# One adaLN chunk computed on TensorE in place of VectorE, and the sine layers of the Hyena filters written ahead of all adaLN work

## The chip, the cores and the metric

The kernel runs on one core of one Trainium2 chip. The metric is device time in microseconds (us) of one launch; lower is better. All times below are device times of that one core.

## The reference, cut to what matters

The program is a two-layer encoder trunk over 256 tokens of width 1024. Every layer is an FFN half-step, a mixer (RWKV-7, Hyena long convolution and Mamba-2 side by side) and a second FFN half-step. Each of the three is modulated by a vector that comes from the conditioning `c`:

```
cond = silu(c)
mod  = (cond @ ada_w[l] + ada_b[l]).reshape(bsz, 1, 9, D_MODEL)
h    = modulate(x, mod[:, :, 0], mod[:, :, 1])          # x * (1 + scale) + shift
x    = layer_norm(ALPHA * x + 0.5 * mod[:, :, 2] * swiglu(h, ...), ...)
```

`ada_w[l]` is 1024 x 9216, so each of the nine chunks of `mod` is a 1024 x 1024 matrix times one vector. Chunk 0 (shift) and chunk 1 (scale) of layer 0 stand before the first FFN.

The Hyena mixer needs a filter for each layer that depends on no activation:

```
hdn = sin(freq[0] * (feats @ f_w1 + f_b1))
hdn = sin(freq[1] * (hdn @ f_w2 + f_b2))
h   = (hdn @ f_w3) * exp(-dist * deltas),  normalised over the tokens, then its spectrum
```

## The kernel before, in words

Activations lie with channels on partitions, 256 tokens in the free dimension. FFN weights are loaded as 128x1024 f32 blocks by SyncE (`dma`, L295), split into two fp32r parts by ScalarE and VectorE (`split`, L308), and each 128x128 piece is multiplied three times (`mm3`, L341). A plain f32 matmul is one call in the code and two MATMUL instructions, each with its own LDWEIGHTS, in the trace.

The program is written for a framework that orders the instructions of each engine itself: every instruction has a priority by its place in the code, and a simulated timeline of the build gives an engine the first instruction by priority among those that are ready in it. The order on an engine is then fixed; on the chip each engine works through its list, and an instruction that waits holds all behind it. So work written later can run earlier, where it was ready earlier in that timeline.

The start of the program, before the first FFN, does four things.

- **The conditioning** (`cond_row`, L404): `c` is broadcast to 128 partitions, goes through Silu, and one row is stored for later use.
- **adaLN chunks 0 and 1** (`ada`, L416, with l=0, sub=0, q=0 and 1): the weights lie with outputs on partitions and the 1024 inputs in the free dimension. For each of eight output blocks a 128x1024 block is loaded, and one VectorE instruction (L433) multiplies it by the broadcast `cond` and sums it into one column of `mod`. At the end of a chunk the bias is added. The eight buffers are four of the tag `raw` and four of the arena, which are taken again for the second chunk.
- **The Hyena filters** (`hy_filter`, L1237): a matmul of the features, a sine layer (`hy_sin`, L1215: six VectorE instructions and a Sin on ScalarE), a matmul, a second sine layer; then for each layer two 512-wide matmuls with a window (`ht`), sixteen instructions of a norm (L1263: 128x128 stationary, 2 columns moving), sixteen 512-wide instructions of the spectrum (L1272), and a store.
- **The modulated input** (`start`, L464): `h = x * (1 + scale) + shift`, split into its parts, for the first FFN.

In the code (L1463 to L1469) chunk 0 comes first, with the constants, the window and the transform matrix loaded after its sixth block; then the filters; then chunk 1. The first FFN (`ffn`, L624) follows.

Of the kernel before, what the change touches and what calls it, by code (L numbers as in the profile page):

```python
# [14 lines left out]
AF = mybir.ActivationFunctionType  # L15
# [41 lines left out]
def layout(inp):  # L57

    f = {k: np.asarray(v) for k, v in inp.items()}
    out = {}  # L60
    c = np.ascontiguousarray
    out["x"] = c(f["x"][0].T.reshape(NT, 128, L).transpose(1, 0, 2))
    out["c"] = c(f["c"])
    out["ada"] = c(f["ada_w"].reshape(DEPTH, 1024, 9, NT, 128).transpose(0, 2, 3, 4, 1))
    out["wi"] = c(f["ffn_wi"].reshape(DEPTH, 2, NT, 128, 2, NF, 128).transpose(0, 1, 5, 4, 3, 2, 6))
    out["wo"] = c(f["ffn_wo"].reshape(DEPTH, 2, NF, 128, NT, 128).transpose(0, 1, 4, 3, 2, 5))
    w = f["mix_w_in"]
    t = lambda a: a.reshape(DEPTH, NT, 128, -1, 128).transpose(0, 3, 2, 1, 4)
    o1, o2, o3 = 1920, 3456, 5008
    out["win"] = c(np.concatenate([t(w[..., :o1]), t(w[..., o1:o2]), t(w[..., o2:o3 - 16]), t(w[..., o3:])], 1))  # L70
    wdt = np.zeros((DEPTH, 128, NT, 64), w.dtype)
    wdt.reshape(DEPTH, 128, NT, 2, 32)[..., :8] = w[..., o3 - 16:o3].reshape(DEPTH, NT, 128, 2, 8).transpose(0, 2, 1, 3, 4)
    out["wdt"] = wdt
    out["pab"] = c(np.stack([f[k].reshape(DEPTH, 4, 128, 4, 2, 128).transpose(0, 3, 2, 4, 1, 5)
                             for k in ("proj_a", "proj_b", "proj_c")], 1))
    out["wout"] = c(f["mix_w_out"].reshape(DEPTH, NT, 128, NT, 128).transpose(0, 3, 2, 1, 4))
    col = lambda a: a.reshape(DEPTH, -1, 128).transpose(0, 2, 1)

    def two(a):
        r = np.zeros((DEPTH, 128, 1), a.dtype)  # L80
        r[:, :64].reshape(DEPTH, 2, 32)[..., :8] = a
        return r

    parts = dict(ada_b=col(f["ada_b"]), lnw=col(f["ln_w"]), lnb=col(f["ln_b"]), mu0=col(f["rw_mu"][:, 0]),
                 mu1=col(f["rw_mu"][:, 1]), w0=col(f["rw_w0"]), a0=col(f["rw_a0"]), kk=col(f["rw_kk"]),
                 ka=col(f["rw_ka"]), rk=col(f["rw_rk"]), lxw=col(f["rw_lnx_w"]), lxb=col(f["rw_lnx_b"]),
                 hcw=col(f["hy_conv_w"]), hcb=col(f["hy_conv_b"]), hbias=col(f["hy_bias"]),
                 scw=col(f["ssd_conv_w"]), scb=col(f["ssd_conv_b"]), D=col(np.repeat(f["ssd_D"], 64, axis=1)),
                 snw=col(f["ssd_norm_w"]), dtb=two(f["ssd_dt_bias"]), alog=two(f["ssd_A_log"]))
    out["par"] = c(np.concatenate([parts[k] for k in COLS], 2))  # L90
    out["w2"] = c(f["rw_w2"].reshape(DEPTH, 128, 512))
    out["a2"] = c(f["rw_a2"].reshape(DEPTH, 128, 512))
    out["g2"] = c(f["rw_g2"])
    flt = np.zeros((128, 708), f["hy_f_w1"].dtype)
    for k in range(DEPTH):
        rows = slice(64 * k, 64 * k + 64)
        flt[:33, 64 * k:64 * k + 64] = f["hy_f_w1"][k]
        flt[rows, 128:192], flt[rows, 192:704] = f["hy_f_w2"][k], f["hy_f_w3"][k]
        for n, a in enumerate((f["hy_f_b1"][k], f["hy_f_b2"][k], f["hy_freq"][k, 0], f["hy_freq"][k, 1])):
            flt[rows, 704 + n] = a  # L100
    out["flt"] = flt
    out.update(constants())
    return out
# [108 lines left out]
class Builder:  # L212
# [203 lines left out]
    def ada(self, l, sub, q):  # L416
        if q == 0 or (l, sub) not in self.mods:
            self.mods[(l, sub)] = self.t("mod", 40, 3)
        m = self.mods[(l, sub)]
        j = 3 * sub + q  # L420
        for b in range(NT):
            n = 8 * q + b
            if self.side:
                raw = self.ring[b % NRING] if self.ring else self.pt("ada_raw", 1024, 3)
            else:
                raw = self.raws[n % len(self.raws)] if 4 <= n < 12 else self.t("raw", 1024, 4)
            self.dma(raw[:], self.ap["ada"][l, j, b])
            if self.ring and SPOOL[b]:
                self.nc.gpsimd.tensor_tensor(out=raw[:], in0=raw[:], in1=self.cond, op=MUL)
                self.act(raw[:], raw[:], AF.Copy, accum_out=m[:, 8 * q + b:8 * q + b + 1])  # L430
                yield
                continue
            self.stt(raw[:], raw[:], 1.0, self.cond, MUL, MUL, accum_out=m[:, 8 * q + b:8 * q + b + 1])  # L433
            yield
        self.tt(m[:, 8 * q:8 * q + 8], m[:, 8 * q:8 * q + 8], self.pc(l, "ada_b", 8 * j, 8), ADD)
        if q == 1:
            self.ts(m[:, 8:16], m[:, 8:16], 1.0, ADD)
        if q == 2:
            self.ts(m[:, 16:24], m[:, 16:24], 0.5, MUL)
        if q == 1 and (l, sub) != (0, 0):  # L440
            pl, psub = (l, sub - 1) if sub else (l - 1, 2)
            w, b = self.pc(pl, "lnw", 8 * psub, 8), self.pc(pl, "lnb", 8 * psub, 8)
            self.tt(m[:, 24:32], w, m[:, 8:16], MUL)
            self.tt(m[:, 32:40], b, m[:, 8:16], MUL)
            self.tt(m[:, 32:40], m[:, 32:40], m[:, 0:8], ADD)
        self.done.add((l, sub, q))
        yield


# [784 lines left out]
        for dst, n in list(zip(self.hc, ("feats", "flt", "win0", "fwd")))[i:i + 2]:  # L1234
            self.dma(dst, ap[n])

    def hy_filter(self):  # L1237

        nc, A, F, bank = self.nc, self.A, self.F, self.bank
        ft, flt, win, fwd = self.hc  # L1240
        h1, h2 = A("hd1", 256), A("hd2", 256)
        rows = [slice(64 * l, 64 * l + 64) for l in range(DEPTH)]
        pb = bank("s", 2)
        self.mm(pb[:, 0:256], flt[0:33, 0:128], ft, True, True)
        self.ts(h1, pb[:, 0:256], flt[:, 704:705], ADD, flt[:, 706:707], MUL)
        self.hy_sin(h1)
        pb = bank("s", 2)
        for r in rows:
            self.mm(pb[r, 0:256], flt[r, 128:192], h1[r], True, True)
        self.ts(h2, pb[:, 0:256], flt[:, 705:706], ADD, flt[:, 707:708], MUL)  # L1250
        self.hy_sin(h2)
        self.hsp = []
        for l, r in enumerate(rows):
            ht, sq = A(f"ht{l}", 2, 512), A("hsq", 2, 512)
            for c in (0, 1):
                pb = bank("m", 2)
                self.mm(pb[:], h2[r, 128 * c:128 * c + 128], flt[r, 192:704], True, True)
                self.tt(ht[:, c, :], pb[:], win[:, c, :], MUL)
            self.act(sq, ht, AF.Square)
            pb = bank("m", 2)  # L1260
            for j in range(4):
                for c in (0, 1):
                    self.mm(pb[:, 2 * j:2 * j + 2], sq[:, c, 128 * j:128 * j + 128], self.ones[:, 0:2], c == 0, c == 1)  # L1263
            rs = self.const(f"hrs{l}", [128, 4])
            self.ts(rs[:], pb[:, 0:8].rearrange("p (a b) -> p a b", b=2)[:, :, 0], 1e-12, ADD)
            self.act(rs[:], rs[:], AF.Sqrt)
            nc.vector.reciprocal(out=rs[:], in_=rs[:])
            hs = A(f"hspec{l}", 4, 512)
            for n, b in enumerate((0, 1, 4, 5)):
                pb = bank("s", 2)  # L1270
                for c in (0, 1):
                    self.mm(pb[:], fwd[:, c, 128 * b:128 * b + 128], ht[:, c, :], c == 0, c == 1)  # L1272
                nc.scalar.copy(out=hs[:, n, :], in_=pb[:])
            d = self.dp.tile([128, 4, 512], F32, tag=f"hsp{l}", bufs=1, name=f"hsp{l}")
            self.dma(d[:], hs)
            self.hsp.append((d, rs))
            F(f"ht{l}", "hsq", f"hspec{l}")
        F("feats", "flt", "win0", "fwd", "hd1", "hd2")
# [166 lines left out]
def build(nc, tc, ap):  # L1445
    with ExitStack() as es:
        b = Builder(nc, tc, ap, es)
        for l in range(DEPTH):
            for sub in range(3):
                with b.phase("p") as b.pp:  # L1450
# [6 lines left out]
                    if (l, sub) == (0, 0):  # L1457
                        with b.phase("s") as pool:
                            b.arena_open((pool, START))
                            b.hy_load(0)  # L1460
                            b.dma(b.par[0][:], b.ap["par"][0])
                            b.raws = [b.A(f"raw{i}", 1024) for i in range(NRAW)]
                            for q in (0, 1):  # L1463
                                for i, _ in enumerate(b.ada(0, 0, q)):
                                    if (q, i) == (0, 5):
                                        b.setup()
                                        b.hy_load(2)
                                if q == 0:
                                    b.hy_filter()  # L1469
                        b.arena = None  # L1470
                    with b.phase("f") as b.pp, b.phase("w") as b.wp, b.phase("l") as b.lp:
# [24 lines left out]
```

## Time and profile before

| | us |
|---|---|
| median of 3 runs | 1669.35 |
| lowest and highest of them | 1665.41, 1672.22 |
| the profiled execution, its own time | 1675.59 |
| span of the profiled execution, first to last instruction | 1673.7 |
| TensorE busy in it | 1569.5 (94%) |
| VectorE busy | 1150.0 (69%) |
| ScalarE busy | 801.3 (48%) |

PE stands for TensorE's matmuls, PEld for its weight loads, DVE for VectorE, ACT for ScalarE, POOL for GpSimd, SP for SyncE with the DMA queue. A busy PE need not be a PE at its peak, since ends of matmuls are modelled. Times in rows are counted from the first instruction of the span.

### The profile page before, as it was taken

How to read it: one execution, taken by the hardware profiler on the slowest of the kernel's cores; microseconds unless marked ns; L12 is line 12 of the kernel's file. 1: busy time of each engine (PE TensorE's matmuls, PEld its weight loads, DVE VectorE, ACT ScalarE, POOL GpSimd, SP SyncE). 2: the span in 40 equal slices, each digit the busy share in tenths (PEclk: the TensorE clock that was granted, in tenths of full speed). 3: DMA queues.
4: the chain of work that ended last, by engine and by line, in shares of the span. 5: the costliest groups of instructions: out<-in, count | busy, mean ns of one | idle time of the engine just before them, and what ended most of it. 6: DMA issues, size and time to landing. Idle time of an engine off the chain costs nothing.

```text
span 1673.7 us, 31929 instructions
## 1 busy us (share of the span) xinstructions
PE 1569.5 (94%) x12118; PEld 1424.0 (85%) x12118; DVE 1150.0 (69%) x2326; ACT 801.3 (48%) x1566; POOL 267.4 (16%) x376
## 2 busy tenths in 40 slices
PE   5999999879998988899999999998999998989996
PEld 2999998768877878899999999877787787989996
DVE  6788856636446677888888887467454557876665
ACT  2655545423243535655575555452424342665554
POOL 0000013567001001100030000348620100030001
PEclk9999999989999999899999999998999999989998
DMA  9898834554548754788869986345555655666663
GB/s 376 305 324 280 282 123 155 129 127 144 169 150 288 242 170 151 282 304 295 266 220 366 315 307 199 120 106 138 156 151 158 223 188 194 189 198 221 222 177 93
DMA packets 157879, 355.74 MB, mean 213 GB/s; under 512 B 55900, under 2 KB 75805, under 8 KB 157470
## 3 DMA queue, kind: packets, MB, share of 16 engines
q1 hardware_dynamic: 157726, 353.71, 64.3%
q8 instruction: 95, 1.56, 0.4%
q14 instruction: 58, 0.48, 0.1%
HBM read 332.11 MB, written 18.91 MB: 210 GB/s over the span
## 4 chain that ended last, share of the span: by engine, by line
PE 66%; DVE 10%; POOL 9%; DMA 7%; ACT 4%; issue 3%; SPq 1%; DVEq 0%; ACTq 0%; POOLq 0%
PE psd L293 57%; PE psm L293 5%; PE pss L293 4%; POOL arena L921 3%; POOL arena L919 3%; DVE arena L282 3%; DVE arena L290 2%; DVE wlo L309 1%; SPq L296 1%; DMA arena<-in_ada 1%; ACT L279 1%; DMA gi<-gate 1%; DMA ada_raw<-in_ada 1%; ACT arena L279 1%; DMA raw<-in_pab 1%
## 5 line engine op out<-in xcount | busy, mean ns | idle before, releaser
L279 ACT ACTIVATE whi<-raw 128x512 fp32r<-128x512 f32 x608 | 370.6, 618 | 328.8 <-PE psd L293 268.2
L309 DVE TENSOR_TENSOR wlo<-raw,whi 128x512 fp32r<-128x512 f32 x608 | 405.1, 676 | 135.1 <-ACT whi L279 120.2
L293 PE MATMUL psd<-hhi,raw 128*128 128x256 f32 x1856 | 435.8, 389 | 0.7 <-DVE arena L290 0.7
L293 PEld LDWEIGHTS psd<-hhi,raw 128*128 128x128 f32 x1856 | 348.9, 192 | 63.3 <-issue 11.6
L293 PE MATMUL psd<-hhi,whi 128*128 128x256 f32 x1360 | 385.4, 285 | 9.9 <-DVE r L290 4.9
L293 PE MATMUL psd<-hhi,wlo 128*128 128x256 f32 x1360 | 384.6, 284 | 1.3 <-DVE wlo L309 1.3
L293 PE MATMUL psd<-hlo,whi 128*128 128x256 f32 x1360 | 385.5, 284 | 0.0
L293 PEld LDWEIGHTS psd<-hhi,whi 128*128 128x128 f32 x1360 | 262.0, 193 | 11.8 <-ACT sg L279 4.6
L293 PEld LDWEIGHTS psd<-hhi,wlo 128*128 128x128 f32 x1360 | 261.9, 193 | 1.6 <-DVE wlo L309 1.5
L293 PEld LDWEIGHTS psd<-hlo,whi 128*128 128x128 f32 x1360 | 262.5, 193 | 0.1
L293 PE MATMUL psd<-alo,whi 128*128 128x256 f32 x704 | 198.7, 282 | 0.0
L293 PE MATMUL psd<-ahi,wlo 128*128 128x256 f32 x704 | 197.8, 281 | 0.0
L293 PE MATMUL psd<-ahi,whi 128*128 128x256 f32 x704 | 197.4, 280 | 0.0
L581 POOL TENSOR_TENSOR r<-r,lmu 128x256 f32<-128x256 f32 x36 | 31.2, 899 | 1020.7 <-ACT lmu L279 841.3
L290 DVE SCALAR_TENSOR_TENSOR ada_raw<-ada_raw,cond 128x1024 f32<-128x1024 f32 x104 | 127.1, 1222 | 20.3 <-DMA ada_raw<-in_ada 20.1
L293 PEld LDWEIGHTS psd<-ahi,wlo 128*128 128x128 f32 x704 | 134.0, 190 | 0.3
L293 PEld LDWEIGHTS psd<-alo,whi 128*128 128x128 f32 x704 | 132.8, 189 | 0.2
L293 PEld LDWEIGHTS psd<-ahi,whi 128*128 128x128 f32 x704 | 132.2, 188 | 0.1
L293 PE MATMUL pss<-arena 128*64 128x128 f32 (+5 forms) x486 | 101.7, 385 | 26.9 <-ACT arena L279 8.6
L279 ACT ACTIVATE arena<-arena 128x512 f32<-128x512 f32 (+4 forms) x108 | 65.8, 619 | 102.5 <-DVE arena L290 35.6
L293 PEld LDWEIGHTS pss<-arena 128*64 128x64 f32 (+3 forms) x486 | 65.4, 195 | 52.1 <-issue 21.0
L293 PE MATMUL psm<-arena 32*32 32x32 f32 (+6 forms) x664 | 64.5, 263 | 28.1 <-DVE arena L290 12.6
(228 smaller groups left out, 2169.9 us busy)
## 6 DMA issues: line engine op xcount, KB each, us to landing
raw<-in_wi SPq DMA_DIRECT2D x176, 512.0 KB, 4.6
raw<-in_win SPq DMA_DIRECT2D x118, 512.0 KB, 3.8
ada_raw<-in_ada SPq DMA_DIRECT2D x104, 512.0 KB, 5.5
raw<-in_wo SPq DMA_DIRECT2D x64, 512.0 KB, 3.8
arena<-in_ada SPq DMA_DIRECT2D x32, 512.0 KB, 5.9
raw<-in_wo SPq DMA_DIRECT2D x32, 384.0 KB, 3.7
raw<-in_pab SPq DMA_DIRECT2D x24, 512.0 KB, 4.3
raw<-in_wout SPq DMA_DIRECT2D x16, 512.0 KB, 4.2
```

Source lines behind the costliest of these rows:

```text
L279: return self.nc.scalar.activation(out=out, in_=in_, func=func, **k)
L282: return self.nc.vector.tensor_tensor(out=out, in0=a, in1=b, op=op)
L290: return self.nc.vector.scalar_tensor_tensor(out=out, in0=a, scalar=s, in1=b, op0=op0, op1=op1, **k)
L293: return self.nc.tensor.matmul(out, lhsT, rhs, start=start, stop=stop, **k)
L296: self.nc.sync.dma_start(out, in_)
L309: return self.act(hi, src, AF.Copy), (eng or self.nc.vector).tensor_tensor(out=lo, in0=src, in1=hi.bitcast(F32), op=SUB)
L581: x = sub_(out=r[:, m, :], in0=r[:, m, :], in1=mu[:], op=SUB)
L919: g.tensor_tensor(out=tv, in0=zw[:, j + 1:32, j:j + 1].to_broadcast([64, n, j]), in1=zw[:, j:j + 1, 0:j].to_broadcast([64, n, j]), op=MUL)
L921: g.tensor_tensor(out=zw[:, j + 1:32, 0:j], in0=zw[:, j + 1:32, 0:j], in1=tv, op=ADD)
```

## The change: what it does

Chunk 0 of layer 0 is taken out of `ada` and done by `ada_first`. A second copy of that chunk's weights lies in memory with the inputs on partitions (`ada0`), and `c` comes once more as columns (`ccol`, each value twice). For each of eight input blocks, a 128x1024 block is loaded, and eight f32 matmuls with 128x128 of it as the stationary operand and two columns of Silu(c) as the moving one add into sixteen columns of one PSUM bank. After the eighth block VectorE adds the bias out of PSUM into `mod`. Chunk 1 stays as it was. The buffers are the same eight, in another order.

`hy_filter` is cut in two: `hy_hidden` (the two matmuls and the two sine layers) is written ahead of all adaLN work, and the rest is written after the fourth block of chunk 1. The constants, the window and the transform matrix are loaded after the fourth block of chunk 0, where it was the sixth.

```
+    out["ada0"] = c(f["ada_w"][0, :, :1024].reshape(NT, 128, 1024))
+    out["ccol"] = c(np.repeat(f["c"].reshape(NT, 128).T[:, :, None], 2, 2))
...
-                raw = self.raws[n % len(self.raws)] if 4 <= n < 12 else self.t("raw", 1024, 4)
+                raw = self.raws[n % len(self.raws)] if n < 12 else self.t("raw", 1024, 4)
...
+    def ada_first(self):
+
+        self.mods[(0, 0)] = m = self.t("mod", 40, 3)
+        cc = self.A("ccol", NT, 2)
+        self.dma(cc, self.ap["ccol"])
+        self.act(cc, cc, AF.Silu)
+        pb = self.bank("d", 4)
+        for k in range(NT):
+            raw = self.raws[k] if k < 4 else self.t("raw", 1024, 4)
+            self.dma(raw[:], self.ap["ada0"][k])
+            for b in range(NT):
+                self.mm(pb[:, 2 * b:2 * b + 2], raw[:, 128 * b:128 * b + 128], cc[:, k, :], k == 0 and b == 0, k == 7,
+                        skip_group_check=True)
+            yield
+        self.tt(m[:, 0:8], pb[:, 0:16].rearrange("p (a b) -> p a b", b=2)[:, :, 0], self.pc(0, "ada_b", 0, 8), ADD)
+        self.done.add((0, 0, 0))
         yield
...
-    def hy_filter(self):
-
-        nc, A, F, bank = self.nc, self.A, self.F, self.bank
-        ft, flt, win, fwd = self.hc
-        h1, h2 = A("hd1", 256), A("hd2", 256)
+    def hy_hidden(self):
+
+        A, bank = self.A, self.bank
+        ft, flt = self.hc[:2]
+        h1, h2 = self.hh = A("hd1", 256), A("hd2", 256)
...
+    def hy_filter(self):
+
+        nc, A, F, bank = self.nc, self.A, self.F, self.bank
+        ft, flt, win, fwd = self.hc
+        h2 = self.hh[1]
...
                             b.raws = [b.A(f"raw{i}", 1024) for i in range(NRAW)]
-                            for q in (0, 1):
-                                for i, _ in enumerate(b.ada(0, 0, q)):
-                                    if (q, i) == (0, 5):
-                                        b.setup()
-                                        b.hy_load(2)
-                                if q == 0:
+                            b.hy_hidden()
+                            for i, _ in enumerate(b.ada_first()):
+                                if i == 3:
+                                    b.setup()
+                                    b.hy_load(2)
+                            for i, _ in enumerate(b.ada(0, 0, 1)):
+                                if i == 3:
                                     b.hy_filter()
```

## Rows read from the trace of the kernel before

**Rows 1.** The page: busy time, share of the span and instructions of each engine.
```profile
PE 1569.5 (94%) x12118; PEld 1424.0 (85%) x12118; DVE 1150.0 (69%) x2326; ACT 801.3 (48%) x1566; POOL 267.4 (16%) x376
```

**Rows 2.** The chain that ended last, 0 to 110 us: start, length, what.
```profile
1.66 5.13 DMA arena<-in_flt
...
8.95 1.23 DVE raw L290 x2
...
57.51 52.57 PE psd L293 x437
```

**Rows 3.** Windows: busy per engine, then granted clock, DMA share, GB/s.
```profile
10.00:20.00 10.00, 1.11 (x4) 0.29 (x4) 9.44 (x24) 0.42 (x1) 0.00 (x0) 1.00 1.03 418
...
30.00:40.00 10.00, 10.00 (x35) 5.03 (x34) 6.89 (x13) 4.59 (x7) 0.00 (x0) 1.00 1.00 401
...
48.00:60.00 12.00, 12.00 (x103) 12.00 (x102) 6.94 (x16) 8.48 (x15) 0.00 (x0) 1.00 0.77 288
...
180.00:200.00 20.00, 20.00 (x172) 19.95 (x171) 17.90 (x38) 11.12 (x23) 0.00 (x0) 1.00 0.84 287
```

**Rows 4.** The timeline of PE, 0 to 48 us: start, length, instructions, what ended a wait.
```profile
6.93 1.19 PE L293 MATMUL pss<-arena 33*128 33x256 f32 x2 [6.93 <-DMA arena<-in_flt]
16.67 1.11 PE L293 MATMUL pss<-arena 64*64 64x256 f32 x4 [8.55 <-ACT arena L279]
21.24 3.77 PE L293 MATMUL psm<-arena 64*128 64x512 f32 x4 [3.46 <-ACT arena L279]
24.95 6.11 PE L293 MATMUL pss<-arena 128*128 128x512 f32 x8
30.90 1.84 PE L293 MATMUL psm<-cst,arena 128*128 128x2 f32 x16
32.67 1.12 PE L293 MATMUL psm<-arena 64*128 64x512 f32 x2
33.72 3.70 PE L293 MATMUL pss<-arena 128*128 128x512 f32 x8
37.35 1.12 PE L293 MATMUL psm<-arena 64*128 64x512 f32 x2
...
46.76 0.80 PE L293 MATMUL psm<-hhi,whi 128*128 128x256 f32 x2
```

**Rows 5.** The timeline of all engines, 0 to 60 us: VectorE and ScalarE.
```profile
8.95 1.22 DVE L290 SCALAR_TENSOR_TENSOR raw<-raw,cond 128x1024 f32<-128x1024 f32 x1
...
17.84 0.54 DVE L287 TENSOR_SCALAR arena<-pss,arena 128x256 f32<-128x256 f32 x1 [0.39 <-PE pss L293]
...
20.77 0.42 ACT L279 ACTIVATE arena<-arena 128x256 f32<-128x256 f32 x1 [4.16 <-DVE arena L287]
...
41.52 0.17 DVE L282 TENSOR_TENSOR mod<-mod,par 128x8 f32<-128x8 f32 x1
```

**Rows 6.** The timeline of PE's weight loads, first at 6.9 us, then 1158 to 1168.
```profile
6.90 0.28 PEld L293 LDWEIGHTS pss<-arena 33*128 33x128 f32 x1 [6.90 <-issue]
...
7.07 0.33 PEld L293 LDWEIGHTS pss<-arena 33*128 33x128 f32 x1
...
1160.30 0.33 PEld L293 LDWEIGHTS pss<-arena 64*128 64x128 f32 x1
...
1160.52 0.33 PEld L293 LDWEIGHTS pss<-arena 64*128 64x128 f32 x1
```

**Rows 7.** Windows around pauses of PE, columns as in rows 3.
```profile
292.00:296.00 4.00, 0.86 (x5) 0.52 (x4) 3.94 (x4) 1.68 (x5) 3.92 (x5) 1.00 0.36 133
296.00:300.00 4.00, 3.62 (x29) 3.50 (x30) 3.92 (x6) 2.06 (x5) 3.84 (x5) 0.57 0.00 0
...
332.00:336.00 4.00, 0.39 (x2) 0.00 (x0) 3.96 (x5) 0.00 (x0) 3.76 (x5) 1.00 0.51 159
...
1160.00:1162.00 2.00, 2.00 (x15) 1.78 (x15) 0.38 (x1) 0.49 (x2) 1.76 (x4) 0.50 0.44 87
```

**Rows 8.** The timeline of PE where it starts again after the first pause.
```profile
295.24 0.71 PE L293 MATMUL psm<-arena 64*128 64x128 f32 x4 [3.09 <-DVE arena L290]
```

More of the change, by code (lines that the diff above doesn't have):

```diff
@@ L446, in ada @@
         self.done.add((l, sub, q))
+        yield
[11 more added lines that the diff above has]
+                        skip_group_check=True)
+            yield
+        self.tt(m[:, 0:8], pb[:, 0:16].rearrange("p (a b) -> p a b", b=2)[:, :, 0], self.pc(0, "ada_b", 0, 8), ADD)
+        self.done.add((0, 0, 0))
         yield
@@ L1251, in hy_filter @@
         self.hy_sin(h2)
+    def hy_filter(self):
+        nc, A, F, bank = self.nc, self.A, self.F, self.bank
+        ft, flt, win, fwd = self.hc
+        h2 = self.hh[1]
+        rows = [slice(64 * l, 64 * l + 64) for l in range(DEPTH)]
         self.hsp = []
```

## The prediction

> **What bounds the kernel now.** I read the page first: PE is busy for 94% of the span, VectorE, the next engine, for 69% [rows 1]. Next the chain of waits over the first 110 us: it begins with the load of the filters' constants, passes through VectorE's adaLN products, goes over to PE, and from 57.51 us it is FFN matmuls alone [rows 2]. The windows say from when PE has no air: between 48 and 60 us it is busy 12.00 of 12.00 us, and still 20.00 of 20.00 at 180 to 200 [rows 3]. So a microsecond by which the first FFN matmul, at 46.76 us [rows 4], moves is a microsecond at the end of the kernel. The question is what sets that 46.76.
>
> PE's timeline answers it. After two small sine matmuls PE starts the filters at 21.24, when the second sine has ended on ScalarE (20.77 + 0.42), and goes through 25.5 us of filter work with one group starting as the former ends, right up to the FFN [rows 4, 5]. Of the two other conditions, shift and scale are complete after the bias add at 41.52 [rows 5], about 5 us before the FFN starts, and ScalarE and VectorE make the split parts of h and weights in between. The DMA engines are full from 10 to 40 us (share 1.00 to 1.03, 401 to 418 GB/s) [rows 3], but nothing at 46.76 waits for them. So the start is bounded by PE: a late start (21.24) plus 25.5 us.
>
> Those 25.5 us hold some slow time. Eight spectrum instructions took 5.95 us from 24.95 to 30.90 and 3.63 us from 33.72 to 37.35; four 64-row ones took 3.71 us from 21.24, where two take 1.05 from 32.67 [rows 4]. The first are at 1.2 GHz, the second at 2.4, whatever the granted clock's column says (1.00 throughout, which I don't trust before the first change). The low level costs 3.71 - 2.10 = 1.6 and 5.95 - 3.63 = 2.3 us, 3.9 together, so the filters at the high level are 25.5 - 3.9 = 21.6 us. A loss of 2.3 us at half speed is 4.6 us of low clock after 24.95: the clock rose at about 29.6, 8.4 us after PE had begun to run without gaps.
>
> **The change part by part.**
>
> *Removed from VectorE:* eight products of 1.22 us [rows 5], 9.8 us. They are not on the path by themselves; VectorE fills 9.44 of 10 us between 10 and 20 [rows 3], and what that delays is the sine chain. From the end of the first sine matmul (6.93 + 1.19 = 8.1) to the second (16.67) 8.5 us pass; the second layer, nearly undisturbed, needs from 17.8 to 21.2, that is 3.4 us [rows 4, 5]. With both layers first, the second sine can be done at 8.1 + 3.4 + 1.1 + 3.4 = 16.0 in place of 21.2. That is the change's gain for the filters: up to 5.2 us, if PE is free then.
>
> *Added to PE:* the chunk's 8 blocks x 8 output groups, each matmul two instructions, are 128 instructions. The trace has their exact form: the norm's 128x128 stationary with two columns moving, where 8 calls in the code are 16 instructions. They took 32.67 - 30.90 = 1.77 us at the high level, 0.111 each [rows 4], so the chunk costs 14.2 us there. At the low level no such row exists. Bounds from weight loads of 128 columns at that level: the first pair starts 0.17 apart (6.90, 7.07) and ends 0.22 apart (7.18, 7.40); a steady stream at a granted clock of 0.50 starts every 0.22 (1160.30, 1160.52), though it has more columns moving [rows 6, 7]. So 21.8 to 28.2 us; I take the steady row, nearest in kind, 0.22 and 28.2.
>
> The Trainium skill (TensorE: Matmul & The Clock Gate, section on LDWEIGHTS) gives a load's time as its columns over 1.2, and names no clock level. By it 128 loads would cost an estimated 13.7 us at either level; the load's records are 0.28 to 0.33 us at the low level, longer than that, so I weigh it only as the second rival.
>
> *Where it lands:* blocks arrive from about 8 us on (VectorE worked on the first at 8.95 [rows 5]) at 0.5 MB each, which at 410 GB/s is 1.28 us. PE needs 16 x 0.111 = 1.8 us a block at the high level and 3.5 at the low. So PE, not the DMA, sets this chunk's pace, and PE's idle time up to 21.24, some 13 us, is filled with about 14 us of work at best and 28 at worst. That is the core: the idle hole is about as long as the work put into it at full clock, and half as long at the low one. PE then has no pause from 8.1 on, so its end is a sum.
>
> At full clock throughout: 8.1 + 0.6 (second sine matmul, half of 1.11) + 14.2 + 21.6 = 44.5, 2.3 us before 46.76; PE is known to begin low, so this is a floor. All of the chunk low, and the filters as low as before: 8.1 + 1.1 + 28.2 + 21.6 + 3.9 = 62.9, 16.1 us late. If instead the last four blocks run beside the filters' wide matmuls and get the high level (7.1 in place of 14.1), 55.9, 9.1 us late. How they are mixed is fixed by the build's own timeline and not to be seen here. I take the middle, 12.6 us.
>
> *Small parts and waits:* the `ccol` load is one small issue on SP, its Silu is 128x16 on a ScalarE that is busy 0.42 of 10 us between 10 and 20 [rows 3], the bias add 0.17 [rows 5]: nothing, under PE's 28 us. On SP the constants, window and transform matrix go ahead of two adaLN blocks that they followed; the bytes up to chunk 1 are the same. Four reloads for chunk 1 now wait until PE has read blocks 0 to 3 (about 23 us at the low level), the other four for blocks 4 to 7; queued behind them on SP are x and the first FFN weights. With the last block read near 40 us, chunk 1 ends near 45 and h some 5 us later, near 50: hidden behind a PE that is busy to 55.9 or longer, and no cost. If PE were done at 47, blocks 4 to 7 would be read before 27, and chunk 1 would end no later than now. VectorE stands behind no new wait: its sine operations lead.
>
> **The rivals.**
>
> *First: the clock rises during the chunk.* After 295.24, following a 3.09 us pause, the clock was 0.57 on average between 296 and 300, so PE was low for about 3.4 us of these and rose some 4.2 us after its new start [rows 7, 8]; at the start of the kernel it took 8.4. With either after 8.1, low running at 0.22 in place of 0.111 loses half of it, 2.1 to 4.2 us: 44.5 + 2.1 to 4.2 = 46.6 to 48.7, so -0.2 to +1.9 us, 1670.2 in the middle. For it: PE is never idle from 8.1 on. Against: PE had no gap between 21.24 and 29.6 either, with matmuls far wider than two columns, and that took twice as long as after 295.24; time without a gap alone doesn't explain the rise. The Trainium skill (same page, Part 1) says that the default is the throttled state and that activity releases it, which read plainly makes this rival the outcome.
>
> *Second: weight loads cost the same at both levels.* Then the chunk is 14.2 us even at the low one: 8.1 + 1.1 + 14.2 + 21.6 + 3.9 = 48.9, 2.1 us late, 1671.5. Against it stand the 0.22 us rows.
>
> *Third, the other side: part of the filters moves behind the FFN.* If the build's timeline finds h ready before the second layer's filter, half of the 21.6 us (10.8) could go behind the first FFN, which has the priority of later code. It gains only if it lands in PE's pauses (3.1 us at 292 to 296, 3.6 at 332 to 336 [rows 7]) and not in the full stretch to 200. With the first rival's clock that is -9 to -11, 1659.4. It decides from about 8.4 us of filter work placed beyond 200 us. Nothing in the order now, filters wholly ahead of the FFN, speaks for it.
>
> That the sine layers gain nothing is part of each sum: PE takes its list in order, and the second sine matmul may stand behind two or three blocks (each 3.5 us low). It costs nothing while PE is busy.
>
> **How the numbers follow.** The profiled execution took 1675.59 us for a span of 1673.7; the median is 1669.35, 6.2 lower, and shifts are added to the median. Likeliest (0.54): +12.6, 1682; its own range, +5.9 (0.17 us a load and the high level for the last four blocks: 8.1 + 1.1 + 10.9 + 7.1 + 21.6 + 3.9 = 52.7) to +19 (the filters' first wide matmuls low for 3 us more of loss), 1675 to 1688. First rival 0.36, second 0.04, third 0.06. The range takes in the first two rivals and leaves out the third and the tails: 1668 to 1688. About what a measurement of this kernel can tell from no change is 0.5%, 8.3 us. A tenth of the likeliest lies below that: slower 0.49, same 0.45 (both rivals and that tenth), faster 0.06.
>
> **What the profile after would show.** Right: a two-column group of 128 matmuls from about 8 us, 0.2 us each or more, with loads of about 0.33; the first FFN matmul at 53 to 65; PE full from there; VectorE's sine operations without products between; h ready well before PE takes it. The first rival: the group's spacing falls to 0.11 on the way, and the FFN starts within 2 us of 46.76. Wrong in any case: an FFN start that doesn't carry over to the end, a chunk paced by its loads, or the FFN waiting for chunk 1's reloads.

## The result, and the profile after

The change made the kernel slower: 1687.53 us (median of four runs, 1685.40 to 1691.09) against 1669.57 (four runs of the kernel before), a ratio of 1.0117 with a 95% interval of 1.0092 to 1.0143. On 1669.35 us that is +19.5 us, between +15.4 and +23.9. I had forecast +12.6 and a range that ended at 1688, and the ratio puts the time at 1688.9. The spans of the two profiled executions differ by 15.6 us (1689.3 and 1673.7). The direction came out as forecast, and so did the low clock on the chunk; the size did not.

The timeline of PE after the change, as in [rows 4] (lines have moved by two: L295 is the former L293):

```profile
6.81 1.19 PE L295 MATMUL pss<-arena 33*128 33x256 f32 x2 [6.81 <-DMA arena<-in_flt]
8.54 6.96 PE L295 MATMUL psd<-arena 128*128 128x2 f32 x32 [0.55 <-DMA arena<-in_ada]
15.43 1.12 PE L295 MATMUL pss<-arena 64*64 64x256 f32 x4
16.47 6.99 PE L295 MATMUL psd<-arena 128*128 128x2 f32 x32
23.32 13.79 PE L295 MATMUL psd<-arena,raw 128*128 128x2 f32 x64
37.05 3.78 PE L295 MATMUL psm<-arena 64*128 64x512 f32 x4
40.75 5.56 PE L295 MATMUL pss<-arena 128*128 128x512 f32 x8
...
50.40 0.68 PE L295 MATMUL psd<-hhi,whi 128*128 128x256 f32 x1
```

The chunk is the second, fourth and fifth of these groups (32, 32 and 64 instructions). Read them against the norm's two-column matmuls in [rows 4], where 16 took 1.77 us (0.111 each). Here the last 64 take 13.73 (37.05 - 23.32): 0.2145 each, and the first 32 take 6.89 (15.43 - 8.54), 0.2153. That is about twice the time at the high level, so all 128 instructions ran at the 1.2 GHz level. Only the four 256-column matmuls of the second sine layer (1.04 us) stand between them, and none of the filters' 512-wide ones. The four 64-row matmuls of the filter behind them still take 3.70 us, as in the kernel before, so PE comes out of 28 us of almost pure two-column work, without a pause, at the same level at which it went in.

The chain that ended last, 0 to 120 us, shows what this does to the FFN:

```profile
8.54 6.96 PE psd L295 x32
15.50 1.05 PE pss L295 x4
16.54 20.57 PE psd L295 x96
37.12 3.71 PE psm L295 x4
40.82 5.49 PE pss L295 x8
...
65.43 5.75 PE psm L295 x48
71.19 48.84 PE psd L295 x407
```

From 8.54 us on the chain is PE alone, each piece beginning where the one before ends. The FFN by itself begins at 65.43; 24 of its matmuls, at about 0.12 us, stand in gaps of the chain's filter pieces before that, so the equivalent start is 65.43 - 2.9 = 62.5, against 46.76 in [rows 4]: 15.7 us late. The timeline of SP shows how much of it is left where the first FFN's rows are written, kernel before, then after:

```profile
249.49 5.85 SPq L296 DMA_DIRECT2D xd<-r  x8
```

```profile
264.59 5.29 SPq L298 DMA_DIRECT2D xd<-r  x8
```

That is 15.1 us, and 15.6 at the end of the span. The windows say why nothing is given back: PE is full from the chunk on (two of them; columns as in [rows 3]).

```profile
20.00:30.00 10.00, 10.00 (x49) 10.00 (x48) 2.96 (x5) 0.00 (x0) 0.00 (x0) 1.00 1.00 395
...
76.00:96.00 20.00, 20.00 (x169) 20.00 (x169) 16.40 (x32) 10.22 (x22) 0.00 (x0) 1.00 1.01 399
```

The granted clock reads 1.00 in the first of these, in a stretch where every instruction takes the low level's time; the column can't be used there, as I said of the kernel before. VectorE and ScalarE on the timeline, as in [rows 5]:

```profile
8.04 0.54 DVE L289 TENSOR_SCALAR arena<-pss,arena 128x256 f32<-128x256 f32 x1 [0.70 <-PE pss L295]
...
10.65 0.29 DVE L289 TENSOR_SCALAR arena<-arena 128x256 f32<-128x256 f32 x1
...
37.16 0.17 DVE L284 TENSOR_TENSOR mod<-psd,par 128x8 f32<-128x8 f32 x1 [2.35 <-PE psd L295]
...
41.51 0.15 DVE L284 TENSOR_TENSOR mod<-mod,par 128x8 f32<-128x8 f32 x1
```

The first sine layer runs from 8.04 to 10.9 with no product between its steps, and both halves of the modulation are complete at 41.7, well before the FFN can start. The page has PE at 95%, with the 128 instructions more, and VectorE at 68%:

```profile
PE 1597.0 (95%) x12246; PEld 1451.6 (86%) x12246; DVE 1141.0 (68%) x2310; ACT 802.4 (48%) x1567; POOL 267.7 (16%) x376
```

### The profile page after: what moved, and what is told of

Its sections match the earlier page's. It is cut to its first block, busy times and chain, and to the rows that moved or that the text cites. A ratio compares the mean times of both kernels' runs of the same rounds, so it can differ in the third digit from the quotient of the medians.

```text
span 1689.3 us, 32179 instructions
## 1 busy us (share of the span) xinstructions
PE 1597.0 (95%) x12246; PEld 1451.6 (86%) x12246; DVE 1141.0 (68%) x2310; ACT 802.4 (48%) x1567; POOL 267.7 (16%) x376
## 4 chain that ended last, share of the span: by engine, by line
PE 68%; DVE 9%; POOL 8%; DMA 7%; ACT 4%; issue 2%; SPq 1%; ACTq 0%; DVEq 0%; POOLq 0%
PE psd L295 59%; PE psm L295 5%; PE pss L295 4%; POOL arena L941 3%; POOL arena L939 3%; DVE arena L284 2%; DVE arena L292 2%; DMA arena<-in_ada 2%; DVE wlo L311 1%; ACT L281 1%; DMA gi<-gate 1%; ACT arena L281 1%; DMA ada_raw<-in_ada 1%; DMA raw<-in_pab 1%; SPq L298 1%
## 5 line engine op out<-in xcount | busy, mean ns | idle before, releaser
L295 PE MATMUL psd<-hhi,raw 128*128 128x256 f32 x1856 | 436.0, 390 | 0.2 <-PE psm L295 0.2
L295 PEld LDWEIGHTS psd<-hhi,raw 128*128 128x128 f32 x1856 | 349.1, 192 | 62.8 <-issue 11.3
L295 PE MATMUL psd<-hhi,whi 128*128 128x256 f32 x1360 | 386.0, 286 | 8.7 <-DVE r L292 4.8
L295 PE MATMUL psd<-hlo,whi 128*128 128x256 f32 x1360 | 385.7, 284 | 0.0
L295 PE MATMUL psd<-hhi,wlo 128*128 128x256 f32 x1360 | 384.3, 284 | 1.1 <-DVE wlo L311 1.1
L295 PEld LDWEIGHTS psd<-hhi,whi 128*128 128x128 f32 x1360 | 261.5, 193 | 10.9 <-ACT whi L281 4.7
L295 PEld LDWEIGHTS psd<-hlo,whi 128*128 128x128 f32 x1360 | 262.3, 193 | 1.5 <-issue 1.2
L295 PEld LDWEIGHTS psd<-hhi,wlo 128*128 128x128 f32 x1360 | 261.6, 193 | 1.6 <-DVE wlo L311 1.3
L295 PE MATMUL psd<-alo,whi 128*128 128x256 f32 x704 | 198.7, 282 | 0.0
L295 PE MATMUL psd<-ahi,wlo 128*128 128x256 f32 x704 | 197.8, 281 | 0.0
L295 PE MATMUL psd<-ahi,whi 128*128 128x256 f32 x704 | 197.4, 280 | 0.0
L295 PEld LDWEIGHTS psd<-ahi,wlo 128*128 128x128 f32 x704 | 134.0, 190 | 0.3
L295 PEld LDWEIGHTS psd<-alo,whi 128*128 128x128 f32 x704 | 132.7, 189 | 0.2
L295 PEld LDWEIGHTS psd<-ahi,whi 128*128 128x128 f32 x704 | 132.2, 188 | 0.1
L295 PE MATMUL pss<-arena 128*64 128x128 f32 (+5 forms) x486 | 101.6, 384 | 20.4 <-DMA arena<-in_flt 6.8
L281 ACT ACTIVATE arena<-arena 128x512 f32<-128x512 f32 (+5 forms) x109 | 66.0, 615 | 96.1 <-DVE arena L292 35.8
L295 PEld LDWEIGHTS pss<-arena 128*64 128x64 f32 (+3 forms) x486 | 65.2, 194 | 43.7 <-issue 20.1
L295 PE MATMUL psm<-arena 32*32 32x32 f32 (+6 forms) x664 | 63.7, 265 | 25.0 <-DVE arena L292 10.6
```

The source lines that it names most:

```text
L281: return self.nc.scalar.activation(out=out, in_=in_, func=func, **k)
L295: return self.nc.tensor.matmul(out, lhsT, rhs, start=start, stop=stop, **k)
```

## The experiments

The theory to be tested: PE begins at 1.2 GHz, a stream of two-column matmuls doesn't bring it to 2.4, and so the chunk costs twice what fits into PE's idle time. Its rivals: the full DMA queues slow the chunk; the place of the sine layers, not the chunk, makes the difference; and, as half of my sum assumed, the low level would have cost less if part of the chunk had run among the filters' wide matmuls. All ratios are to the kernel before, timed on the same chip.

**The sine layers first, and nothing else.** The chunk goes back to VectorE:

```diff
 b.hy_hidden()
-for i, _ in enumerate(b.ada_first()):
-...
+for q in (0, 1):
+    for i, _ in enumerate(b.ada(0, 0, q)):
+        if (q, i) == (0, 5):
+            b.setup()
+            b.hy_load(2)
+    if q == 0:
+        b.hy_filter()
```

> One half of the change alone: both sine layers written ahead of all adaLN work, chunk 0 back on VectorE with its old buffers and the old places of the loads and of the rest of the filters. My theory (the 128 two-column instructions on PE at the low clock are the whole loss): the second sine is done at 16 to 18 us in place of 21.2, the filters start 3 to 5 us earlier, and the kernel is 2 to 5 us faster than before, near 1665. Rival A (the new order of the sine layers is what costs): no faster than before, and slower if it carries the loss, up to 1687.

Measured: 1668.26 us (12 runs), ratio 0.9989 (0.9973 to 1.0005). The gain did not come, and PE's timeline says why:

```profile
16.66 1.12 PE L295 MATMUL pss<-arena 64*64 64x256 f32 x4 [8.55 <-ACT arena L281]
21.24 3.78 PE L295 MATMUL psm<-arena 64*128 64x512 f32 x4 [3.46 <-ACT arena L281]
```

These are the times of [rows 4]. The instructions of VectorE and of PE stand in the same order as before: the build goes by data that are ready, and the products' data are ready while a sine step waits. Writing the layers first changes nothing, and my expectation of 2 to 5 us was wrong.

**The sine layers first, enforced.** `hy_sin` returns its last VectorE instruction, and each product of the chunk is ordered behind it, the first behind the first layer, the others behind the second:

```diff
-            self.stt(raw[:], raw[:], 1.0, self.cond, MUL, MUL, accum_out=...)
+            x = self.stt(raw[:], raw[:], 1.0, self.cond, MUL, MUL, accum_out=...)
+            if (l, sub, q) == (0, 0, 0):
+                self.after(x, self.sines[b > 0])
...
```

> Chunk 0 on VectorE as before, and the sine layers really first: the first product is ordered behind the last VectorE step of the first sine layer, all further ones behind that of the second (order on the engine only). My theory: the second sine is done at 16 to 17 us in place of 21.2, PE begins the filters 4 to 5 us earlier and ends them near 42, and the FFN starts there or when h is ready, 42 to 44: 3 to 5 us faster than before, 1665 to 1667. Rival (shift and scale, whose products now begin later on VectorE, become the bound): h ready at 47 or later, 1670 or slower.

Measured: 1666.25 us (12 runs), ratio 0.9981 (0.9967 to 0.9995). PE's timeline:

```profile
15.04 3.78 PE L295 MATMUL psm<-arena 64*128 64x512 f32 x4 [3.46 <-ACT arena L281]
21.06 6.22 PE L295 MATMUL pss<-arena 128*128 128x512 f32 x8 [2.24 <-DVE arena L284]
...
42.98 0.80 PE L295 MATMUL psm<-hhi,whi 128*128 128x256 f32 x2
```

The filters begin 6.2 us sooner and the FFN 3.8 sooner; between, PE waits 2.24 us for a filter step that now stands behind products on VectorE. This is what the change's second part gives when it is enforced: some 3 us, 0.2% (0.8 to 5.5 us by the interval).

**The chunk on PE, and the sine layers not ahead of it.** The whole filter code is written behind the chunk:

```diff
-b.hy_hidden()
 for i, _ in enumerate(b.ada_first()):
-    if i == 3:
+    if i == 5:
         b.setup()
         b.hy_load(2)
+b.hy_hidden()
+b.hy_filter()
 for i, _ in enumerate(b.ada(0, 0, 1)):
-    if i == 3:
-        b.hy_filter()
+    pass
```

> The other half alone: chunk 0 on TensorE as in the change, the filters written whole behind it as before, their loads after the sixth block. My theory: the chunk again takes about 27.6 us on PE at 0.215 us an instruction, the second sine matmul and so the filters come after it at 38 to 42 us, and the kernel is 15 to 19 us slower than before, 1685 to 1689. Rival A: no slower than before, 1670.

Measured: 1692.80 us (four runs), ratio 1.0136 (1.0104 to 1.0168). PE's timeline:

```profile
22.03 13.79 PE L295 MATMUL psd<-arena,raw 128*128 128x2 f32 x64
35.75 1.11 PE L295 MATMUL pss<-arena 64*64 64x256 f32 x4
44.16 0.58 PE L295 MATMUL psd<-hhi,whi 128*128 128x256 f32 x1 [7.29 <-ACT whi L281]
```

The chunk alone carries the loss. The second sine matmul now stands behind all of the chunk, and PE then has nothing for 7.29 us; the change's order spares it that. The first FFN's rows are written at 273.15 us, 8.6 us later than with the whole change, so the place of the sine layers helps once the chunk is there; in the time (1692.80 against 1687.53, with intervals that overlap) this isn't shown.

**A clock already high when the chunk begins.** Eight wide instructions on a tile of ones, their result unused, are put on PE while it waits for the first load:

```diff
+    def warm_up(self, n):
+        w = self.A("wu", 512)
+        self.nc.vector.memset(w, 1.0)
+        pb = self.bank("d", 4)
+        for i in range(n):
+            self.mm(pb[:], w[:, 0:128], w, True, True)
...
+b.warm_up(4)
 b.hy_hidden()
```

> The changed kernel with four f32 matmuls of 128x512 ones (eight instructions, result not used) on PE before the first data arrive, so that PE has run for some 7 us when the chunk begins. My theory (it is the clock's level that doubles the chunk): the two-column instructions start at 0.111 us; if the level holds, the chunk takes 14 us in place of 27.6 and the kernel comes to 1674 to 1677; if the level falls within the chunk, the spacing goes back to 0.215 at that point and the time lies between that and 1687. Rival B (the weight loads read from buffers while the DMA engines are full, and that makes them 0.215 apart at any level): 0.215 from the first block on, 1686 to 1689.

Measured: 1686.78 us (four runs), ratio 1.0100 (1.0071 to 1.0129). The windows:

```profile
10.00:12.00 2.00, 2.00 (x18) 2.00 (x18) 0.29 (x1) 0.42 (x1) 0.00 (x0) 0.87 1.03 418
12.00:14.00 2.00, 2.00 (x11) 2.00 (x11) 0.23 (x1) 0.00 (x0) 0.00 (x0) 0.50 1.04 421
```

This is the most telling pair of rows. PE is busy 2.00 of 2.00 us in both, with the same instructions; 18 of them fit before and while the clock falls and 11 after it. So the stream doesn't merely fail to raise the clock: a high level is lost while it runs, with no pause from 8.33 us on. Ahead of 8.33 PE had waited 0.97 us for the first block. That wait alone hardly explains the loss: in the kernel before, PE waits 1.43 us in the stretch from 580 to 584 us, with 256-column matmuls before and after it, and the granted clock stays at 1.00:

```profile
580.00:582.00 2.00, 0.77 (x5) 0.37 (x3) 2.00 (x5) 0.12 (x1) 0.00 (x0) 1.00 1.01 351
582.00:584.00 2.00, 1.78 (x14) 1.76 (x15) 0.95 (x3) 1.13 (x3) 0.00 (x0) 1.00 0.99 366
```

In the two rows of this run the DMA share is 1.03 and 1.04, and yet the first holds 18 instructions and the second 11, so the full DMA queues are not what slows them. The first FFN's rows are written 2.7 us sooner than with the change alone.

**The same chunk with 128 equal columns moving.** The weights, their loads and the number of instructions stay; the two columns become 128 copies of one, in two accumulators:

```diff
-pb = self.bank("d", 4)
+cw = self.A("cwide", NT, 128)
+for k in range(NT):
+    self.act(cw[:, k, :], cc[:, k, 0:1].to_broadcast([128, 128]), AF.Copy)
+pbs = [self.bank("d", 4) for _ in (0, 1)]
...
-self.mm(pb[:, 2 * b:2 * b + 2], raw[:, 128 * b:128 * b + 128], cc[:, k, :], k == 0 and b == 0, k == 7,
-        skip_group_check=True)
+self.mm(pbs[b // 4][:, 128 * (b % 4):128 * (b % 4) + 128], raw[:, 128 * b:128 * b + 128], cw[:, k, :],
+        k == 0 and b % 4 == 0, k == 7, skip_group_check=True)
```

> The changed kernel with 128 equal columns of Silu(c) moving in place of two, into two banks; weights, loads and their number are unchanged, and eight copies on ScalarE widen the columns. The build puts the first filter matmuls between the last four blocks. My theory: an instruction takes the same 0.21 us at the low level (a matmul of 128 columns fits under the load), but PE now raises its clock on the way, after 4 to 9 us, and the rest runs at 0.111: the chunk's share of PE falls from 27.6 to 17 to 21 us and the kernel to 1677 to 1682. Rival B: 0.215 all the way, 1687 or later.

Measured: 1668.86 us (10 runs), ratio 0.9992 (0.9974 to 1.0009). The whole loss is gone, with more columns to compute. Windows of this kernel, then the same stretches of the changed one:

```profile
10.00:12.00 2.00, 2.00 (x11) 2.00 (x11) 1.01 (x3) 0.42 (x1) 0.00 (x0) 1.00 1.03 419
12.00:14.00 2.00, 2.00 (x14) 2.00 (x13) 0.23 (x1) 0.00 (x0) 0.00 (x0) 1.00 1.03 414
...
16.00:18.00 2.00, 2.00 (x20) 2.00 (x19) 1.83 (x6) 0.00 (x0) 0.00 (x0) 1.00 1.02 416
```

```profile
10.00:12.00 2.00, 2.00 (x11) 2.00 (x11) 0.87 (x3) 0.42 (x1) 0.00 (x0) 1.00 1.01 413
12.00:14.00 2.00, 2.00 (x11) 2.00 (x10) 0.23 (x1) 0.00 (x0) 0.00 (x0) 1.00 1.05 426
...
16.00:18.00 2.00, 2.00 (x12) 1.53 (x8) 1.30 (x4) 0.00 (x0) 0.00 (x0) 1.00 1.02 418
```

Count the instructions in the parentheses, since the clock's column is blind here: both kernels put 11 into 10 to 12 us; then the 128-column chunk rises to 14 and 20, before a single 512-wide filter matmul has run (the first comes at 19.02), and the two-column one stays at 11 and 12. What differs on PE up to there is the columns moving and, with them, that the results go to two accumulators in place of one; no run parts these two. The gain is larger than the 1677 to 1682 that I expected, because I had counted the chunk alone (it takes 17.0 us of PE here, 10.5 less). The filters then find the high level too, which is the 3.9 us of the prediction's sum, and the first FFN's rows are written at 249.78 us, 14.8 sooner than in the changed kernel.

**Both: 128 columns and wide instructions ahead.** The two edits above together.

> The run with 128 columns moving, and eight wide instructions on PE ahead of it as in the run e3. My theory (PE's time before the FFN is a sum of work at the level of the clock, and 128 columns hold the level that two columns let fall): the clock is high when the chunk begins and stays high, the chunk takes 14 to 15 us, the filters 21.6, and the FFN starts 2 to 3 us earlier than in the run without the wide instructions: 1664 to 1667. Rival (the level falls within the chunk here too, whatever the columns): as that run or later, 1668 to 1675.

Measured: 1670.16 us (10 runs), ratio 1.0011 (0.9998 to 1.0024): no gain. Its timelines of PE and SP:

```profile
45.38 1.88 PE L295 MATMUL pss<-arena 128*128 128x512 f32 x4
46.69 0.68 PE L295 MATMUL psm<-hlo,whi 128*128 128x256 f32 x1
```

```profile
248.09 4.82 SPq L298 DMA_DIRECT2D xd<-r  x8
```

PE is at the high level from the chunk on. The last filter matmul ends at 46.7, with 10 FFN matmuls (1.2 us) done before, so the equivalent FFN start is 45.5, 1.3 us ahead of 46.76, and 1.4 us are there at the first FFN's rows. So the 1664 to 1667 that I expected did not come: even at full clock this chunk has next to nothing to win: it fills PE's idle time almost exactly. The time shows none of these 1.4 us. In the profiled executions this run is still ahead of the run with 128 columns alone at the third last writing of such rows (1060.11 against 1064.44 us), yet its span is 3.1 us longer (1672.4 and 1669.3); what comes after is the same code, and I haven't settled where it goes.

**Wide instructions around the enforced sine layers**, with the chunk on VectorE: four calls ahead of the first sine matmul, three behind it, four behind the second, each on ones and unused.

```diff
+wide = lambda n, *prev: [self.after(self.mm(wb[:], w[:, 0:128], w, True, True), *prev) for _ in range(n)]
+wide(4)
-self.mm(pb[:, 0:256], flt[0:33, 0:128], ft, True, True)
+wide(3, self.mm(pb[:, 0:256], flt[0:33, 0:128], ft, True, True))
...
+wide(4, x)
...
```

> The run before, with wide matmuls of ones (result not used) on PE before the first sine matmul, between the two and after the second, so that PE is at its high clock when the filters begin. My theory: the filters take 21.6 us in place of 25.5 and end near 39; the FFN then starts when h is ready, 40 to 43, 4 to 6 us faster than before, 1664 to 1666. Rival: h is the bound already without the wide matmuls, and nothing more is won than in the run before.

Measured: 1664.69 us (8 runs), ratio 0.9980 (0.9966 to 0.9993), no better than without them. The timeline of PE:

```profile
16.84 1.98 PE L295 MATMUL psm<-arena 64*128 64x512 f32 x4 [0.56 <-ACT arena L281]
22.73 6.08 PE L295 MATMUL pss<-arena 128*128 128x512 f32 x8 [3.90 <-DVE arena L284]
```

The first filter group does go at the high level (1.98 us in place of 3.78), but then PE waits 3.90 us for VectorE, and the next eight take 6.08 again: the clock is lost in the wait (the windows give 0.59 for 20 to 24 us). VectorE is what this start is short of.

**Part of the chunk among the filters' wide matmuls.** This is the case to which I gave half the weight in my sum. In the changed kernel, order edges put one block of the last four (eight calls, 16 instructions) behind every two wide calls (four instructions) of the first layer's spectrum:

```diff
             for b in range(NT):
-                self.mm(...)
+                x = self.mm(...)
+                if k >= 4 and b == 0:
+                    self.after(x, self.prev)
+            self.prev = x
...
                 for c in (0, 1):
-                    self.mm(pb[:], fwd[...], ht[:, c, :], c == 0, c == 1)
+                    x = self.mm(pb[:], fwd[...], ht[:, c, :], c == 0, c == 1)
+                    if c == 0 and l == 0:
+                        self.after(x, self.prev)
...
```

> The changed kernel with the last four blocks of the chunk put, by order edges, between the eight wide 128x512 matmuls of the first layer's filter: one block of eight two-column instructions behind every two wide ones. This is the mixing for which the prediction gave half credit between +16.1 us (whole chunk at 1.2 GHz) and +9.1 us (last four blocks at 2.4 GHz between the filters' matmuls). If mixing brings the high level to those blocks, their 32 instructions go at 0.111 us instead of 0.2155 (-3.3 us) and the first filter's matmuls lose their low-clock surplus (3.7 us): 1678 to 1682 us. The rival: wide matmuls alternating with runs of two-column ones don't raise the clock, the 32 instructions stay near 0.2155 us and the time stays with the change's, 1685 to 1690.

My text counts calls where it says instructions: four blocks are 64 instructions, so 6.7 us rather than 3.3 would have been saved, and 1675 to 1679 us expected in that case; the verdict is the same by either figure. Measured: 1691.65 us (four runs), ratio 1.0134 (1.0111 to 1.0157), above the range of either case. PE's timeline, then SP's where the first FFN's rows are written:

```profile
26.53 3.78 PE L295 MATMUL pss<-arena 128*128 128x512 f32 x4
30.10 3.41 PE L295 MATMUL psd<-arena,raw 128*128 128x2 f32 x16
...
50.44 3.76 PE L295 MATMUL pss<-arena 128*128 128x512 f32 x4
53.99 3.41 PE L295 MATMUL psd<-arena,raw 128*128 128x2 f32 x16
57.33 3.78 PE L295 MATMUL psm<-arena 64*128 64x512 f32 x4
```

```profile
274.23 5.39 SPq L298 DMA_DIRECT2D xd<-r  x8
```

Mixing did the opposite of what I had credited it with. The two-column instructions stay at 0.21 us, and the wide ones are held low with them: four take 3.78 and 3.76 us, where eight take 3.70 at the high level [rows 4]. The first FFN's rows come 9.6 us later than with the change (264.59). PE is still low at 57.33 us, where the 64-row group takes 3.78, nearly 50 us after it began to work without a pause.

**The same, mixed finely:** four two-column calls behind each wide one, about as much PE time in either kind.

```diff
-                if k >= 4 and b == 0:
+                if k >= 4 and b % 4 == 0:
                     self.after(x, self.prev)
-            self.prev = x
+                self.prev = x
...
```

> As the run before, with finer mixing: four two-column instructions behind each of the eight wide matmuls of the first filter, so about as much PE time in the one kind as in the other throughout. If the low level depends on how long two-column instructions run by themselves, this one rises where the mixing by blocks doesn't: 1678 to 1682 us. If half the time in two-column instructions is too much however it is cut, both stay at 1685 to 1690 us. If both rise, the half credit of the prediction was only not taken up by the order that was built.

Measured: 1694.78 us (four runs), ratio 1.0141 (1.0114 to 1.0169), again above the range of either case. PE's timeline:

```profile
54.38 2.05 PE L295 MATMUL pss<-arena 128*128 128x512 f32 x2
56.23 1.71 PE L295 MATMUL psd<-arena,raw 128*128 128x2 f32 x8
57.86 3.78 PE L295 MATMUL psm<-arena 64*128 64x512 f32 x4
```

The wide ones are low here too (two in 1.85 us). Both mixing runs begin at the low level; whether such a mix would keep a high level that it found, no run shows. How finely the two are cut makes no difference that these intervals can tell.

## Why the prediction was right and where it failed

*What bounds the kernel* held: PE's list, in order. The FFN start moved by 15.7 us, the first FFN's rows by 15.1, the end by 15.6.

*Two columns at the low level* held. I took 0.22 us an instruction from weight-load rows of another stage [rows 6, 7] and 28.2 us for the chunk; it took 0.215 and 27.5. That a row with more columns moving gave the right spacing is what the 128-column run bears out: at the low level it too puts 11 instructions into 10 to 12 us. The all-low sum was 62.9 for the FFN start, +16.1; the equivalent start is 62.5. That sum was right to half a microsecond, with a little luck: the chunk was 0.7 us shorter than 28.2, and began 0.4 us later than 8.1.

*The step that failed is "I take the middle, 12.6 us".* I had two ends, +16.1 with all of the chunk low and +9.1 with its last four blocks at the high level among the filters, and no row that chose between them. Two things were wrong with the lower end. The order that was built has none of the filters' wide matmuls within the chunk, so there was nothing to mix. And the two mixing runs show that this end doesn't exist at these proportions for a PE that begins low: mixing keeps the filters low as well, and the medians are 4 and 7 us above the change's, with intervals that overlap its own. The term should have been +16.1, which gives 1685.5 and a range from there; the measured interval, +15.4 to +23.9, holds +16.1 and not +12.6. The median moved a little more than the sum, by 18.0 us where the profiled spans moved by 15.6; that rest is within what executions of one kernel differ by, and no run here tells it apart.

*The first rival* (the clock rises during the chunk, 0.36) didn't come true, and the 128-column run shows that its figures were sound for another stream: there the rise comes between 12 and 14 us and the time is 1668.86, where the rival had 1670.2. Its error was to let PE's being busy stand for what raises the clock. My objection to it, that time without a gap alone doesn't explain the rises in [rows 4, 7, 8], was the right one and should have weighed more. The rule of the Trainium skill that I set beside it (TensorE: Matmul & The Clock Gate, Part 1), that activity releases the throttle, is not borne out in the plain reading: 28 us of two-column matmuls without a gap didn't release it, and with wide instructions ahead such a stream lost the level.

*The second rival* (loads cost the same at both levels, 0.04) falls: 0.111 us in rows of the high level and 0.215 in those of the low. The estimate from the Trainium skill (same page, section on LDWEIGHTS), 13.7 us for the chunk, is half of the 27.5 that was measured.

*The third rival* (filter work behind the FFN) came true in a small, harmless form: 24 FFN matmuls slipped in among the filters, both in the full stretch, so nothing was won.

*The sine layers* I had called a gain of up to 5.2 us if PE is free. PE was not; the second layer ended at 19.96 on ScalarE, against 21.19 before, and the filters started at 37.05 whatever it did. With the chunk on VectorE, the new place of the code changes nothing, and enforced it is worth about 3 us.

*A small reading that was wrong* is that VectorE stands behind no new wait: it waited 2.35 us for the chunk's last result before the bias add at 37.16, and the last two products of chunk 1 came behind that, at 37.42 and 39.76. It cost nothing, since chunk 1 was complete at 41.7, where I had 45.

## What to carry to other kernels

Before you move work into an engine's idle time, price it at the clock that the engine has there. Here the idle stretch was one in which TensorE was at its low level, and a stream with two columns moving did not lift it. Where a stream of small matmuls must run early, try it with more columns, even useless ones: here 128 in place of two removed all of an 18 us loss. And when a sum has two ends and no row that chooses, find out which order the build will take, or keep both ends as cases; the middle of two cases is a time that neither gives.

## What the runs showed of the hardware that I had not expected

- A stream of two-column matmuls with 128x128 weights, PE busy 2.00 of 2.00 us, let the granted clock fall from 1.00 to 0.50 between 10 and 14 us (the run with wide instructions ahead). The same stream with 128 columns went from the low level's pace to the high one's between 12 and 14 us.
- Between such streams wide matmuls stay low too: four of 128x512 take 3.55 us from start to next start (50.44 to 53.99, blocks mixed in), 0.89 each, against 0.45 at the high level (3.63 for eight [rows 4]), with no pause on PE for 42 us.
- The weight-load records follow the clock: on average 332 and 333 ns in the chunk as changed, all low; 192 ns in the later half of the 128-column chunk, all high. A load's record is longer than the spacing of the instructions (0.215 and 0.111 us), so loads overlap.
